# Output projections by seven products: the weights' sums on VectorE and stored in two parts, sums of y partly by accumulating DMAs, y loaded by the GpSimd queue

## The chip, the cores and the metric

One core of a Trainium2 chip runs the whole program. It has five engines, each with its own queue of instructions that it works through in order: TensorE (PE, with PEld for its weight loads), VectorE (DVE), ScalarE (ACT), GpSimd (POOL) and SyncE (SP). The metric is the time of one execution in microseconds; the median of three runs is quoted.

## The reference, cut to what matters

Two pre-norm residual layers on x of 1024 tokens by 1024 channels, and a final norm. Each ends in one projection of 2048 channels to 1024:

```
# layer 0: two branches, concatenated, one output projection
y_a = u * sg * silu(za)                            # gMLP, channels 0..1023
y_b = (layernorm(ht * sigmoid(og)) + skip * xc) * silu(zb)   # mLSTM, 1024..2047
x = x + concatenate([y_a, y_b], axis=-1) @ w_out
# layer 1: differential attention with 16 heads of 128 channels
o = rmsnorm(o, subln_g) * (1 - lam_init)
x = x + (o.reshape(seq, 2048) * silu(z)) @ w_out
return rmsnorm(x, final_g)
```

## The kernel before, in words

Every fp32 product is made of three passes on TensorE: an operand is split into a high part (a cast on ScalarE, L94) and a low part (a subtraction on VectorE, L95), and high by high, low by high and high by low are added. A tile of weights is loaded raw from memory (`wr`, L72) by SP's queue, 512 KB at a time into two buffers, and split into `wh` and `wl`. A matmul of 128x512 follows the one before it after about 0.23 us at the full clock, and after 0.43 us at half of it.

Both output projections are done by seven products of half size instead of eight (Winograd's form of Strassen's scheme). The activations are held as tiles `a[half, k, i]`, each 128x1024: half is the token half, k the channel half, i one of four pairs of 128 channels. Written for short, a11 is half 0, k 0; a21 is half 1, k 0; a12 is half 0, k 1; a22 is half 1, k 1. The products run in the order 1, 7, 2, 6, 5, 3, 4, and each takes 96 matmuls of 128x512. Product 1 needs a11; 7 needs s3 = a11 − a21 (L338); 2 needs a12; 6 needs a21 + a22 − a11 (L341, L342), 5 a21 + a22, 3 a12 less that (L344), 4 a22. These sums run on GpSimd. The weights' sums (products 7, 6, 5, 4) depend on the weights alone: `wout_sums` makes them on GpSimd during layer 0's gMLP stage (L292 to L295) from `wb` tiles that SP's queue loads (L290), and GpSimd's queue stores them to memory (`td`, L297). The output projections load them back through L72 like other weights, and split them there.

In layer 0 the activations lie in memory (`yd`): channels 0 to 1023 are stored by the gMLP stage, channels 1024 to 2047 by the tail of the mLSTM (L1118). In layer 1 they are the heads' outputs (`wd`), and each is multiplied on VectorE (L330) by a row of scales that is loaded into 128 partitions (`yr`, L329, two buffers). Part of product 1 runs, in each layer, as a filler in gaps of the stage before. Product 1's result p (`p`, evacuated at L372) is added to the accumulator tiles `xa` on GpSimd (L398, L400), as soon as those are loaded with the residual (L389).

The gMLP stage goes by eight groups of 128 channels, twice: u (L1187, and the spatial matmul sp, L1190, which needs the normalised va of L1174; the result `yu` at L1192 and L1195), and za (L1207, L1208). Its matmuls stand at L133. A call of `wout_sums` stands behind every second group in the code.

A scheduler reorders all instructions, so the order on an engine is not that of the code; what stands in an engine's queue, and what it waits for, is fixed when the kernel is built. Each DMA that GpSimd issues waits for one of eight slots, that is for the DMA eight places ahead of it in that queue. `SLOTS` says at which of an attention head's steps the last two heads run fillers; once these are done, the fillers of the output projection come.

Of the kernel before, what the change touches and what calls it, by code (L numbers as in the profile page):

```python
# [9 lines left out]
F32 = mybir.dt.float32  # L10
F32R = mybir.dt.float32r
# [3 lines left out]
ALU = mybir.AluOpType  # L15
# [3 lines left out]
P = 128  # L19
# [6 lines left out]
AH, BH, CH = 8, 4, 16  # L26
# [8 lines left out]
SLOTS = {14: (0, 5, 6, 7), 15: (1, 3, 4, 6)}  # L35
# [9 lines left out]
class Trunk:  # L45
# [106 lines left out]
    def run(self):  # L152
        tc, nc, io = self.tc, self.nc, self.io
        with tc.tile_pool(name="const", bufs=1) as cp, \
# [41 lines left out]
            w = self.load_w(io["wO"][1], w0, 1)  # L196
# [18 lines left out]
            w = [self.next_w(), None]  # L215
# [35 lines left out]
            odd.release()  # L251
            self.xp = pool("x3acc", side="right")
            p = pool("wout1b")
            self.wout_rest(p)
            self.wout_p1()
            self.wout_evac(7)
            for i in range(4):
                for k in range(2):
                    self.wout_load(p, k, 1, (i,))
# [24 lines left out]
    def wout_sums(self, pool, layer, i):  # L284

        nc, sub = self.nc, ALU.subtract
        b11, b12, b21, b22 = (pool.tile([P, 1024], F32, name=f"wb{j}", tag=f"wb{j}") for j in range(4))
        t2 = pool.tile([P, 1024], F32, name="wt2", tag="wt2")
        for j, b in enumerate((b11, b12, b22, b21)):
# [27 lines left out]
    def wout_load(self, pool, half, k, pairs):  # L317

        nc = self.nc
        hs = slice(half * 512, (half + 1) * 512)  # L320
        for i in pairs:
            x = self.a[half, k, i] = pool.tile([P, 2, 512], F32, name=f"a{half}{k}{i}")
            for n in range(2):
                nc.sync.dma_start(out=x[:, n], in_=(self.y if self.layer == 0 else self.w)[8 * k + 2 * i + n][:, hs])
            if self.layer == 1:
                r = self.ytmp.tile([P, 2, 512], F32, name="yr", tag="t3", bufs=2)
                for n in range(2):
                    kb = 8 * k + 2 * i + n
                    nc.sync.dma_start(out=r[:, n], in_=self.rr[kb:kb + 1, hs].broadcast_to([P, 512]))  # L329
                nc.vector.tensor_tensor(out=x, in0=x, in1=r, op=ALU.mult)  # L330

    def wout_lhs(self, n, i):

        g, sub = self.nc.gpsimd.tensor_tensor, ALU.subtract
# [10 lines left out]
        return {1: a11, 2: a12, 3: a12, 4: a22, 5: a21, 6: a11}[n]  # L345

# [7 lines left out]
    def wout_prod(self, n, tiles=range(4), groups=((0,), (1,), (2,), (3,))):  # L354

        x = "A" if n in (1, 2, 5, 3) else "B"
        for grp in groups:
            parts = []
            for i in grp:
                w = self.load_w(self.wsrc[n][i])  # L360
                parts.append((i, self.split_y(self.wout_lhs(n, i)), [a.rearrange("p (k c) -> p k c", k=2) for a in w]))
# [758 lines left out]
    def gmlp(self, new_pool):  # L1120
# [56 lines left out]
        wsp = new_pool("w_sums", side="right")  # L1177
        yu = []
        for g in range(AH):
# [16 lines left out]
            if g % 2:  # L1196
                self.wout_sums(wsp, 0, g // 2)
        ap.release()
        mixa = new_pool("mixa")
        for g in range(AH):  # L1200
# [9 lines left out]
            if g % 2:  # L1210
                self.wout_sums(wsp, 1, g // 2)
# [88 lines left out]
```

## Time and profile before

| | |
|---|---|
| median of 3 runs | 2244.39 us (2243.82 to 2246.65) |
| profiled execution | 2249.3 us, of which span 2247.5 us |
| TensorE busy | 2103.8 us, 94% |
| VectorE busy | 1537.3 us, 68% |
| ScalarE busy | 998.0 us, 44% |
| GpSimd busy | 415.6 us, 18% |
| granted TensorE clock, mean | 0.964 |

The profile is of one execution. The span is what the trace covers; 1.8 us of the time lie outside it. The page cuts the span into 40 slices of 56.2 us and gives a tenth per slice: slices 3 to 6 hold the gMLP stage (129 to 355 us), slices 14 to 16 layer 0's output projection (from about 760 us), slices 36 to 40 that of layer 1. "Busy" of the TensorE counts a matmul's whole passage, which overlaps with the next one's.

### The profile page before, as it was taken

What the parts mean: (1) busy time and instruction counts of PE and PEld (TensorE: products, weight loads), DVE (VectorE), ACT (ScalarE), POOL (GpSimd) and SP (SyncE); (2) the same over time, 40 slices, a digit from 0 to 9 for tenths busy, and PEclk for the clock granted to TensorE, in tenths of its full rate; (3) what the DMA queues carried; (4) which work ended last, traced back from release to release, by engine and by line L of the source; (5) the groups of instructions that cost most, each with busy time, mean ns of one, the idle gap of its engine ahead of it and who ended that gap; (6) DMA issues with size and microseconds to landing.
All of it is one profiled execution on the core that took longest, in us unless ns stands there. A gap on an engine that the chain in (4) does not pass through costs nothing. (4 is left out here: it accounts for less than half of the span.)

```text
span 2247.5 us, 32307 instructions
## 1 busy us (share of the span) xinstructions
PE 2103.8 (94%) x11594; PEld 1803.5 (80%) x11594; DVE 1537.3 (68%) x3113; ACT 998.0 (44%) x1943; POOL 415.6 (18%) x427
## 2 busy tenths in 40 slices
PE   8889799999999859999999999999999999997398
PEld 7878688988989737878888888888888888876286
DVE  6363324577777777657777777777777777888665
ACT  5411113343434423544555555555555555663143
POOL 0065600000000273101111111111111111114810
PEclk9989899999999969999999999999999999998699
DMA  4456632121123443445443444454444444347523
GB/s 165 144 208 230 212 117 97 39 71 48 62 66 99 159 168 112 139 132 143 120 119 100 116 115 120 112 130 105 114 115 111 113 124 114 90 146 242 183 95 122
DMA packets 109749, 281.81 MB, mean 125 GB/s; under 512 B 21348, under 2 KB 22276, under 8 KB 109588
## 3 DMA queue, kind: packets, MB, share of 16 engines
q1 hardware_dynamic: 89972, 225.07, 33.4%
q0 software_dynamic: 19616, 54.68, 7.6%
q8 instruction: 91, 1.49, 0.3%
q14 instruction: 70, 0.57, 0.1%
HBM read 168.32 MB, written 44.20 MB: 95 GB/s over the span
## 5 line engine op out<-in xcount | busy, mean ns | idle before, releaser
L133 PE MATMUL un<-hh,wh 128*128 128x512 f32 x1240 | 493.8, 398 | 15.7 <-ACT u L1187 14.5
L133 PE MATMUL un<-hh,wl 128*128 128x512 f32 x1240 | 493.5, 398 | 1.6 <-DVE wl L95 1.6
L133 PE MATMUL un<-hl,wh 128*128 128x512 f32 x1240 | 490.6, 396 | 0.0
L95 DVE TENSOR_TENSOR wl<-wr,wh 128x1024 fp32r<-128x1024 f32 (+1 forms) x191 | 262.1, 1374 | 207.3 <-ACT wh L94 197.8
L94 ACT CAST wh<-wr 128x1024 fp32r<-128x1024 f32 (+1 forms) x191 | 199.8, 1048 | 283.2 <-PE un L133 174.7
L133 PEld LDWEIGHTS un<-hh,wh 128*128 128x128 f32 x1240 | 235.7, 190 | 63.0 <-ACT u L1187 15.3
L133 PEld LDWEIGHTS un<-hh,wl 128*128 128x128 f32 x1240 | 235.1, 190 | 52.4 <-DVE wl L95 2.8
L133 PEld LDWEIGHTS un<-hl,wh 128*128 128x128 f32 x1240 | 235.1, 190 | 48.2
L643 ACT ACTIVATE p<-p,mn 128x128 f32<-128x128 f32 (+7 forms) x256 | 197.7, 774 | 121.1 <-DVE mn L640 120.8
L640 DVE CUSTOM_DVE_ANT_0 p<-S,mask 128x128 f32<-128x128 f32 (+7 forms) x256 | 184.8, 750 | 3.4 <-PE tp L667 1.9
L148 PE MATMUL un<-wh,hh 128*128 128x256 f32 (+1 forms) x560 | 161.4, 289 | 5.0 <-ACT wh L94 3.0
L148 PE MATMUL un<-wl,hh 128*128 128x256 f32 (+1 forms) x560 | 160.2, 286 | 0.9 <-DVE wl L95 0.8
L148 PE MATMUL un<-wh,hl 128*128 128x256 f32 (+1 forms) x560 | 160.2, 286 | 0.4 <-DVE hl L95 0.4
L366 PE MATMUL wps<-wh,yh 128*128 128x512 f32 x320 | 128.3, 406 | 18.2 <-ACT yh L94 15.1
L366 PE MATMUL wps<-wl,yh 128*128 128x512 f32 x320 | 129.8, 406 | 9.2 <-DVE wl L95 9.0
L95 DVE TENSOR_TENSOR yl<-a,yh 128x1024 fp32r<-128x1024 f32 x56 | 85.1, 1521 | 70.3 <-ACT yh L94 70.1
L94 ACT CAST yh<-a 128x1024 fp32r<-128x1024 f32 x56 | 58.6, 1047 | 165.6 <-PE wps L366 130.7
L694 POOL DMA_DIRECT2D wd<-wt x64 | 36.7, 574 | 510.2 <-DVE wt L692 485.6
L366 PE MATMUL wps<-wh,yl 128*128 128x512 f32 x320 | 128.7, 403 | 1.1 <-DVE yl L95 1.1
L95 DVE TENSOR_TENSOR PT<-tp,PT 128x512 fp32r<-128x512 f32 (+1 forms) x192 | 106.0, 552 | 33.0 <-ACT PT L94 32.9
L681 PE MATMUL O<-PT,Vh 128*128 128x512 f32 x320 | 113.7, 388 | 0.5 <-ACT mr L707 0.5
L148 PEld LDWEIGHTS un<-wh,hh 128*128 128x128 f32 x560 | 108.4, 194 | 6.5 <-ACT wh L94 3.2
(339 smaller groups left out, 4698.4 us busy)
## 6 DMA issues: line engine op xcount, KB each, us to landing
wr<-wO SPq DMA_DIRECT2D x79, 512.0 KB
wr<-wE SPq DMA_DIRECT2D x46, 512.0 KB
wr<-td SPq DMA_DIRECT2D x32, 512.0 KB
sw<-xs SPq DMA_DIRECT2D x256, 64.0 KB
Qh<-xh SPq DMA_DIRECT2D x128, 128.0 KB
Ql<-xl POOLq DMA_DIRECT2D x128, 128.0 KB, 4.0
td<-wb POOLq DMA_DIRECT2D x24, 512.0 KB, 5.9
wb<-wF SPq DMA_DIRECT2D x16, 512.0 KB
```

The lines of the kernel that those rows point to most:

```text
L94: return (self.nc.scalar.copy(out=out_h, in_=src).ins, self.nc.vector.tensor_tensor(out=out_l, in0=src, in1=out_h.bitcast(F32), op=ALU.sub ...
L95: self.nc.vector.tensor_tensor(out=out_l, in0=src, in1=out_h.bitcast(F32), op=ALU.subtract).ins)
L133: nc.tensor.matmul(out=ps, lhsT=a[:, kb, :], rhs=b[:, kb, :], start=(kb == 0 and i == 0), stop=(kb == KB - 1 and i == 2))
L148: nc.tensor.matmul(out=ps, lhsT=a[:, k0 + k, sl], rhs=b, start=start and k == i == 0, stop=stop and k == n - 1 and i == 2)
L366: self.nc.tensor.matmul(out=self.wps[x, t], lhsT=y[a][:, k, t * P:(t + 1) * P], rhs=w[b][:, k, :], start=n in (1, 7, 5) and i == k == j == ...
L640: nc.vector.tensor_tensor_reduce(out=p[:, :W], in0=S[:, :W], in1=self.mask[:, T - W:], scale=-0.125, scalar=1e30, op0=ALU.add, op1=ALU.min ...
L643: nc.scalar.activation(out=p[:, :W], in_=p[:, :W], func=AF.Exp, scale=-1.0, bias=mn, accum_out=s)
L681: mm(out=O.rearrange("p (a t) -> p a t", a=2)[:, :, a0:], lhsT=Vh, rhs=pt, start=s == 0, stop=False)
L694: nc.gpsimd.dma_start(out=self.w[h][:, js], in_=wt)
```

## The change

- `wout_sums`: 16 calls with half tiles (128x512) instead of 8 with whole ones, one behind every group; the four sums run on VectorE (L300 after) instead of GpSimd, and each sum is split at once into its high and low part (ScalarE and VectorE, L94 and L95), which are stored as two tiles of 256 KB each (L304). What is stored doubles, from 16.8 to 33.5 MB. The weights' loads go to GpSimd's queue (L289, 256 KB each, two buffers).
- `wout_rhs`: products 7, 6, 5 and 4 load the two parts (L363, 512 KB each) straight into the buffers of `wh` and `wl`, or into a pair of raw ones, and split nothing.
- the sums of y: s3 on VectorE; a21 + a22 and a12 + a11 by DMAs that add to their destination (`accum_op`, L349, L351; 512 KB each, four of each in a layer); a11 − (a21 + a22) on VectorE, with the sign turned so that the next is a sum.
- product 1's p is added to `xa` by twelve accumulating DMAs of 256 KB in each layer (L415) instead of eight GpSimd instructions.
- y's loads (L333) go by GpSimd's queue, but for layer 1's a11 and a21, which stay on SP's; the scales `yr` (L337) go by GpSimd's.
- the order of these steps in the code, and `SLOTS`.

```diff
-SLOTS = {14: (0, 5, 6, 7), 15: (1, 3, 4, 6)}
+SLOTS = {14: (0, 3, 5, 6, 7), 15: (1, 3, 4)}
...
-            self.td = [[dp.tile([4, P, 1024], F32, name=f"td{l}{j}") for j in range(4)] for l in range(2)]
+            self.td = [[dp.tile([4, 2, P, 1024], F32, name=f"td{l}{j}") for j in range(4)] for l in range(2)]
...
             self.wout_load(p, 1, 0, range(4))
+            self.wout_load(p, 0, 1, range(3))
             self.wout_rest(p)
+            self.wout_ps(range(4), "B")
             self.wout_p1()
-            for k in (1, 0):
-                self.wout_load(p, k, 1, range(3))
-            self.wout_ps(range(4), "B")
             run(self.wout_prod(7))
-            for k in (0, 1):
-                self.wout_load(p, k, 1, (3,))
+            self.wout_load(p, 0, 1, (3,))
+            self.wout_load(p, 1, 1, range(4))
...
+    def wout_fetch(self, pool, n):
...
+            for j in (0, 1, 3, 2):
+                self.nc.gpsimd.dma_start(out=self.wb[j], in_=src[4 * j + n % 8 // 2][:, cs])
+
+    def wout_sums(self, pool, n):
...
-            nc.sync.dma_start(out=b, in_=self.io["wF" if layer == 0 else "wG"][4 * (0, 1, 3, 2)[j] + i])
-        g = nc.gpsimd.tensor_tensor
-        g(out=b11, in0=b12, in1=b11, op=sub)
-        g(out=t2, in0=b22, in1=b11, op=sub)
-        g(out=b12, in0=b22, in1=b12, op=sub)
-        g(out=b21, in0=b21, in1=t2, op=sub)
-        for j, b in enumerate((b11, t2, b12, b21)):
-            nc.gpsimd.dma_start(out=self.td[layer][j][i], in_=b)
+        b11, b12, b21, b22 = self.wb
+        self.wout_fetch(pool, n + 1)
...
+        v = nc.vector.tensor_tensor
+        for j, (out, x, y, op) in enumerate(((b11, b12, b11, sub), (t2, b11, b22, sub), (b12, b22, b12, sub), (b21, b21, t2, ALU.add))):
+            v(out=out, in0=x, in1=y, op=op)
+            parts = [pool.tile([P, 512], F32R, name=f"wt{x}", tag=f"wt{x}", bufs=3) for x in "hl"]
+            self.split2(*parts, out)
+            for x, part in enumerate(parts):
+                nc.gpsimd.dma_start(out=self.td[n // 8][j][n % 8 // 2, x][:, cs], in_=part.bitcast(F32))
...
+        q = nc.sync if k == 0 and self.layer == 1 else nc.gpsimd
...
-                nc.sync.dma_start(out=x[:, n], in_=(self.y if self.layer == 0 else self.w)[8 * k + 2 * i + n][:, hs])
+                q.dma_start(out=x[:, n], in_=(self.y if self.layer == 0 else self.w)[kb + n][:, hs])
...
-                    nc.sync.dma_start(out=r[:, n], in_=self.rr[kb:kb + 1, hs].broadcast_to([P, 512]))
+                    nc.gpsimd.dma_start(out=r[:, n], in_=self.rr[kb + n:kb + n + 1, hs].broadcast_to([P, 512]))
...
-            g(out=s3, in0=a11, in1=a21, op=sub)
+            v(out=s3, in0=a11, in1=a21, op=sub)
             return s3
         if n == 6:
-            g(out=a21, in0=a21, in1=a22, op=ALU.add)
-            g(out=a11, in0=a21, in1=a11, op=sub)
-        if n == 3:
-            g(out=a12, in0=a12, in1=a11, op=sub)
+            g(out=a21, in_=a22, accum_op=ALU.add)
+            v(out=a11, in0=a11, in1=a21, op=sub)
+            g(out=a12, in_=a11, accum_op=ALU.add)
...
+    def wout_rhs(self, n, i):
+
+        src = self.wsrc[n][i]
+        if n in (1, 2, 3):
+            w = self.load_w(src)
+        else:
+            w = [self.wp.tile([P, 1056], F32R, name="wr", tag="r4", bufs=2)[:, :1024] if i == 1 else
+                 self.wp.tile([P, 1024], F32R, name=x, tag=x, bufs=2) for x in ("wh", "wl")]
+            for x, part in zip(w, (src[0], src[1])):
+                self.nc.sync.dma_start(out=x.bitcast(F32), in_=part)
...
-        g, add = self.nc.gpsimd.tensor_tensor, ALU.add
         for t in range(4):
-            x = self.xa[t + 4].rearrange("p (a c) -> p a c", a=2)
-            g(out=x, in0=x, in1=self.p1[t].unsqueeze(1).broadcast_to([P, 2, 512]), op=add)
-            x = self.xa[t][:, 512:]
-            g(out=x, in0=x, in1=self.p1[t], op=add)
+            for x in (self.xa[t][:, 512:], self.xa[t + 4][:, 512:], self.xa[t + 4][:, :512]):
+                self.nc.gpsimd.dma_start(out=x, in_=self.p1[t], accum_op=ALU.add)
...
-            if g % 2:
-                self.wout_sums(wsp, 0, g // 2)
+            self.wout_sums(wsp, g)
```

On SP's queue in the gMLP stage of layer 0, before; `wb` are the raw tiles for the weights' sums, `wr` the weights of the stage's own groups:

```order
L290 DMA wb_1841<-wF 128x1024
L290 DMA wb_2009<-wF 128x1024
L72 DMA wr<-wE 128x1024
L290 DMA wb_2006<-wF 128x1024
L290 DMA wb_2007<-wF 128x1024
L290 DMA wb_2008<-wF 128x1024
L72 DMA wr<-wE 128x1024
L290 DMA wb_2176<-wF 128x1024
```

And the same stretch of SP's queue after:

```order
L856 DMA dw<-gw 32x128
L866 DMA eb<-dnM 128x1024
L853 DMA decB<-ddec 128x32
L866 DMA eb<-dnM 128x1024 x3
L72 DMA wr<-wE 128x1024 x20
```

Before, three or four `wb` loads stand ahead of each weight load of a group; after, the weight loads stand alone, and the `wb` loads are on GpSimd's queue, among the stores of the sums. On VectorE's queue of the changed kernel the first four calls' sums stand ahead of the last of the normalisations that make va (here `av`; `wt`, `wtl` are a sum and its low part):

```order
L300 TENSOR_TENSOR wb_1829<-wb_1830,wb_1829 128x512
L65 TENSOR_TENSOR ar_t<-ar_t,ar_h 128x8
L95 TENSOR_TENSOR wtl<-wb_1719,wth 128x512
L66 SCALAR_TENSOR_TENSOR ar_y<-ar_t,ar_y 128x8
L300 TENSOR_TENSOR wt_1949<-wb_1829,wb_1832 128x512
L64 TENSOR_TENSOR ar_t<-ar_y 128x8
L300 TENSOR_TENSOR wb_1830<-wb_1832,wb_1830 128x512
L65 TENSOR_TENSOR ar_t<-ar_t,ar_h 128x8
L95 TENSOR_TENSOR wtl<-wb_1829,wth 128x512
L66 SCALAR_TENSOR_TENSOR ar_y<-ar_t,ar_y 128x8
L300 TENSOR_TENSOR wb_1831<-wb_1831,wt_1949 128x512
L1189 TENSOR_SCALAR av_255<-av_255,amv,ar_y 128x1024
```

Before, nothing of `wout_sums` is on VectorE; from the first piece of the third call to the first `av` now stand thirteen pieces of 128x512 that were not there. On GpSimd's queue at layer 0's output projection, before (`p` is product 1's result, `yd_79` and `yd_80` are the last channels of the mLSTM, `s` is s3):

```order
L400 TENSOR_TENSOR xa_7375<-xa_7375,p_7104 128x512
L398 TENSOR_TENSOR xa_7380<-xa_7380,p_7344 128x1024
L400 TENSOR_TENSOR xa_7376<-xa_7376,p_7344 128x512
L398 TENSOR_TENSOR xa_7381<-xa_7381,p_7352 128x1024
L400 TENSOR_TENSOR xa_7377<-xa_7377,p_7352 128x512
L1118 DMA yd_79<-xc 128x512
L1118 DMA yd_80<-xc 128x512
L338 TENSOR_TENSOR s_7429<-a_6499,a_7362 128x1024
```

After, at the same place (`a_7818` to `a_7827` are a21):

```order
L415 DMA xa_7841<-p_7800 128x512
L415 DMA xa_7845<-p_7800 128x512 x2
L415 DMA xa_7842<-p_7808 128x512
L415 DMA xa_7846<-p_7808 128x512
L1133 DMA yd_79<-xc 128x512
L415 DMA xa_7846<-p_7808 128x512
L1133 DMA yd_80<-xc 128x512
L333 DMA a_7818<-yd_65 128x512
L333 DMA a_7818<-yd_66 128x512
L333 DMA a_7821<-yd_67 128x512
```

The twelve additions are DMAs now, and a21's loads, which stood on SP's queue behind four loads of `td`, stand behind them and behind the last two stores of `yd`. On SP's queue in layer 1's output projection, before, the last five of the 25 rows from product 1's last weights to those of product 2:

```order
L329 DMA yr<-rrd 128x512 x2
L324 DMA a_20856<-wd_8642 128x512
L324 DMA a_20856<-wd_8643 128x512
L329 DMA yr<-rrd 128x512 x2
L72 DMA wr<-wG 128x1024 x4
```

After:

```order
L407 DMA xa_21231<-x2d 128x1024
L407 DMA xa_21227<-x2d 128x1024
L409 DMA gB<-fg 128x1024
L72 DMA wr<-wG 128x1024 x4
L363 DMA wr<-td_87 128x1024 x2
```

The weights of product 2 now stand right behind the residual's loads; a12, a22 and their `yr` are on GpSimd's queue.

## Rows read from the trace of the kernel before

**Rows 1.** The page's slices: PE's busy tenths.

```profile
PE   8889799999999859999999999999999999997398
```

**Rows 2.** Windows of the gMLP stage: length; each engine's busy us (instructions); clock; DMA.

```profile
129.00:151.00 22.00, 15.01 (x50) 11.08 (x49) 19.39 (x26) 0.98 (x2) 12.62 (x8) 0.69 0.64 232
151.00:211.00 60.00, 60.00 (x301) 49.99 (x300) 26.63 (x23) 10.71 (x15) 37.03 (x23) 1.00 0.57 198
211.00:272.00 61.00, 46.50 (x194) 37.35 (x194) 19.39 (x16) 7.49 (x10) 32.47 (x21) 0.86 0.69 239
...
190.00:200.00 10.00, 10.00 (x53) 8.40 (x52) 4.32 (x5) 2.14 (x3) 1.20 (x1) 1.00 1.01 357
```

**Rows 3.** Waits of 129 to 355 us: us in total, times, longest.

```profile
ACT wh L94 <- DMA wr<-wE: 51.9, 3, 20.3
```

**Rows 4.** Timeline of SP's queue there: start, duration, instruction.

```profile
240.09 20.23 SPq L290 DMA_DIRECT2D wb<-wG  x4
```

**Rows 5.** Timeline of VectorE there.

```profile
135.09 12.36 DVE L1174 TENSOR_SCALAR av<-av,amv,ar_y 128x1024 f32<-128x1024 f32 x8
```

**Rows 6.** Groups by line, 129 to 355 us: count, busy us, mean ns, idle.

```profile
L1195 DVE TENSOR_TENSOR yu<-yu,u 128x512 f32<-128x512 f32 x16 | 22.5, 1407 | 1.7
...
L292 POOL TENSOR_TENSOR wb<-wb,wb 128x1024 f32<-128x1024 f32 x7 | 16.6, 2368 | 65.2 <-DMA wb<-wG 37.5 <-DMA wb<-wF 27.7
```

**Rows 7.** Timeline of PE in layer 0's projection, with the idle time before.

```profile
773.00 0.50 PE L366 MATMUL wps<-wl,yh 128*128 128x512 f32 x1 [4.25 <-DVE wl L95]
...
810.28 0.80 PE L366 MATMUL wps<-wh,yh 128*128 128x512 f32 x1 [15.10 <-ACT yh L94]
```

**Rows 8.** Windows there, of L366's matmuls alone: PE, PEld, clock, DMA.

```profile
800.00:844.50 44.50, 28.86 (x97) 22.17 (x98) 0.72 0.55 196
...
820.00:830.00 10.00, 10.00 (x44) 7.98 (x43) 1.00 0.28 95
```

**Rows 9.** Timeline there: VectorE, GpSimd, SP's queue.

```profile
785.46 7.24 DVE L1106 TENSOR_SCALAR og<-og,mv,lr_y 128x256 f32<-128x256 f32 x4
...
794.05 0.69 DVE L1117 TENSOR_TENSOR xc<-xc,zb 128x512 f32<-128x512 f32 x1
...
785.29 2.36 POOL L398 TENSOR_TENSOR xa<-xa,p 128x1024 f32<-128x1024 f32 x1 [11.21 <-ACT p L372]
...
798.01 0.54 POOL L1118 DMA_DIRECT2D yd<-xc  x1 [2.41 <-DVE xc L1117]
...
777.66 21.53 SPq L72 DMA_DIRECT2D wr<-td  x4
799.29 5.60 SPq L324 DMA_DIRECT2D a<-yd  x8
```

**Rows 10.** Timeline of PE in layer 1's projection, with the idle time before.

```profile
2116.86 1.22 PE L366 MATMUL un<-wh,yh 128*128 128x512 f32 x2 [34.32 <-ACT wh L94]
2122.33 0.80 PE L366 MATMUL un<-wl,yh 128*128 128x512 f32 x1 [4.24 <-DVE wl L95]
```

**Rows 11.** Windows there, of L366 alone.

```profile
2033.00:2082.00 49.00, 39.05 (x155) 30.61 (x156) 0.86 0.68 236
...
2116.50:2146.90 30.40, 25.79 (x102) 20.45 (x103) 0.85 0.26 86
2146.90:2247.00 100.10, 89.76 (x380) 71.68 (x378) 0.96 0.31 111
```

**Rows 12.** Timeline of SP's queue there.

```profile
2072.66 0.91 SPq L324 DMA_DIRECT2D a<-wd  x2
...
2110.04 15.91 SPq L72 DMA_DIRECT2D wr<-wG  x4
```

**Rows 13.** DMA issues: KB each, median us from issue to landing.

```profile
Ql<-xl POOLq DMA_DIRECT2D x128, 128.0 KB, 4.0
td<-wb POOLq DMA_DIRECT2D x24, 512.0 KB, 5.9
```

**Rows 14.** Windows of layer 1's first loads, all engines as in Rows 2.

```profile
2010.00:2020.00 10.00, 6.81 (x22) 5.36 (x23) 8.99 (x22) 5.09 (x14) 1.08 (x2) 0.66 0.99 326
```

More of the change, by code (lines that the diff above doesn't have):

```diff
@@ L251, in run @@
             odd.release()
+            p = pool("wout1b")
             self.xp = pool("x3acc", side="right")
-            p = pool("wout1b")
+            self.wout_load(p, 0, 1, range(4))
             self.wout_rest(p)
             self.wout_p1()
+            self.wout_load(p, 1, 1, range(4))
             self.wout_evac(7)
-            for i in range(4):
-                for k in range(2):
-                    self.wout_load(p, k, 1, (i,))
             for n in (2, 6, 5, 3):
@@ L276, in run @@
             self.wp.release()
-    def wout_sums(self, pool, layer, i):
-        nc, sub = self.nc, ALU.subtract
-        b11, b12, b21, b22 = (pool.tile([P, 1024], F32, name=f"wb{j}", tag=f"wb{j}") for j in range(4))
-        t2 = pool.tile([P, 1024], F32, name="wt2", tag="wt2")
-        for j, b in enumerate((b11, b12, b22, b21)):
-            nc.sync.dma_start(out=b, in_=self.io["wF" if layer == 0 else "wG"][4 * (0, 1, 3, 2)[j] + i])
-        g = nc.gpsimd.tensor_tensor
-        g(out=b11, in0=b12, in1=b11, op=sub)
-        g(out=t2, in0=b22, in1=b11, op=sub)
-        g(out=b12, in0=b22, in1=b12, op=sub)
-        g(out=b21, in0=b21, in1=t2, op=sub)
-        for j, b in enumerate((b11, t2, b12, b21)):
-            nc.gpsimd.dma_start(out=self.td[layer][j][i], in_=b)
+    def wout_fetch(self, pool, n):
+        if n < 16:
+            src = self.io["wF" if n < 8 else "wG"]
+            cs = slice(n % 2 * 512, (n % 2 + 1) * 512)
+            self.wb = [pool.tile([P, 512], F32, name=f"wb{j}", tag=f"wb{j}", bufs=2) for j in range(4)]
+            for j in (0, 1, 3, 2):
+                self.nc.gpsimd.dma_start(out=self.wb[j], in_=src[4 * j + n % 8 // 2][:, cs])
+    def wout_sums(self, pool, n):
+        nc, sub = self.nc, ALU.subtract
+        b11, b12, b21, b22 = self.wb
+        self.wout_fetch(pool, n + 1)
+        cs = slice(n % 2 * 512, (n % 2 + 1) * 512)
+        t2 = pool.tile([P, 512], F32, name="wt2", tag="wt2")
+        v = nc.vector.tensor_tensor
[5 more added lines that the diff above has]
+                nc.gpsimd.dma_start(out=self.td[n // 8][j][n % 8 // 2, x][:, cs], in_=part.bitcast(F32))
     def wout_start(self, layer, pool):
@@ L320, in wout_load @@
         hs = slice(half * 512, (half + 1) * 512)
+        q = nc.sync if k == 0 and self.layer == 1 else nc.gpsimd
         for i in pairs:
             x = self.a[half, k, i] = pool.tile([P, 2, 512], F32, name=f"a{half}{k}{i}")
+            kb = 8 * k + 2 * i
             for n in range(2):
-                nc.sync.dma_start(out=x[:, n], in_=(self.y if self.layer == 0 else self.w)[8 * k + 2 * i + n][:, hs])
+                q.dma_start(out=x[:, n], in_=(self.y if self.layer == 0 else self.w)[kb + n][:, hs])
             if self.layer == 1:
@@ L327, in wout_load @@
                 for n in range(2):
-                    kb = 8 * k + 2 * i + n
-                    nc.sync.dma_start(out=r[:, n], in_=self.rr[kb:kb + 1, hs].broadcast_to([P, 512]))
+                    nc.gpsimd.dma_start(out=r[:, n], in_=self.rr[kb + n:kb + n + 1, hs].broadcast_to([P, 512]))
                 nc.vector.tensor_tensor(out=x, in0=x, in1=r, op=ALU.mult)
     def wout_lhs(self, n, i):
-        g, sub = self.nc.gpsimd.tensor_tensor, ALU.subtract
+        g, v, sub = self.nc.gpsimd.dma_start, self.nc.vector.tensor_tensor, ALU.subtract
         a11, a21, a12, a22 = (self.a.get((h, k, i)) for k in range(2) for h in range(2))
@@ L337, in wout_lhs @@
             s3 = self.ytmp.tile([P, 2, 512], F32, name="s3", tag="t3", bufs=2)
-            g(out=s3, in0=a11, in1=a21, op=sub)
+            v(out=s3, in0=a11, in1=a21, op=sub)
             return s3
         if n == 6:
-            g(out=a21, in0=a21, in1=a22, op=ALU.add)
-            g(out=a11, in0=a21, in1=a11, op=sub)
-        if n == 3:
-            g(out=a12, in0=a12, in1=a11, op=sub)
+            g(out=a21, in_=a22, accum_op=ALU.add)
+            v(out=a11, in0=a11, in1=a21, op=sub)
+            g(out=a12, in_=a11, accum_op=ALU.add)
         return {1: a11, 2: a12, 3: a12, 4: a22, 5: a21, 6: a11}[n]
+    def wout_rhs(self, n, i):
[7 more added lines that the diff above has]
+                self.nc.sync.dma_start(out=x.bitcast(F32), in_=part)
+        return [x.rearrange("p (k c) -> p k c", k=2) for x in w]
     def split_y(self, raw):
@@ L359, in wout_prod @@
             for i in grp:
-                w = self.load_w(self.wsrc[n][i])
-                parts.append((i, self.split_y(self.wout_lhs(n, i)), [a.rearrange("p (k c) -> p k c", k=2) for a in w]))
+                parts.append((i, self.split_y(self.wout_lhs(n, i)), self.wout_rhs(n, i)))
             for t in tiles:
@@ L1177, in gmlp @@
         wsp = new_pool("w_sums", side="right")
+        self.wout_fetch(wsp, 0)
         yu = []
@@ L1209, in gmlp @@
             nc.gpsimd.dma_start(out=self.y[g], in_=yu[g])
-            if g % 2:
-                self.wout_sums(wsp, 1, g // 2)
+            self.wout_sums(wsp, AH + g)
         wsp.release()
```

## Prediction

> **What bounds the kernel now.** I read the page's slices first, to see where TensorE pauses, and then for each such stretch the windows, the waits and the timelines of the queues. TensorE is busy nine tenths or more nearly everywhere, and three of its dips lie where the change works [rows 1]. So the question is how much time TensorE loses in three places, and how much of that goes.
>
> *The gMLP stage.* From 151 to 211 us TensorE is full: 301 matmuls in 60.0 us, 5.0 per us. At that pace the 50 matmuls of 129 to 151 us are 10 us of work, and the 194 of 211 to 272 us are 39 us [rows 2]: 12 and 22 us are lost. The 22: ScalarE waits three times, 51.9 us in all, for a group's own weights [rows 3]. They are late because SP's queue stood for 20.23 us at four loads of `wb` [rows 4], whose buffers GpSimd's sums still held, and the next weight load stands behind those. The 12: eight normalisations of va take 12.36 us on VectorE, and the spatial matmul needs them all [rows 5]. GpSimd takes 2.37 us per sum, and VectorE's products of 128x512 take 1.41 us in the mean of this stage [rows 6]; with GpSimd idle one takes 0.69 [rows 9].
>
> *Layer 0's projection.* TensorE stalls 4.25 us at 773 us for a low part, and 15.10 us before product 7 starts at 810.28 [rows 7]. At full clock 44 matmuls pass in 10 us, 0.227 us each; so the 97 of 800 to 844.5 us are 22.0 us of work, and 22.5 us are lost, at a mean clock of 0.72 [rows 8]. On the queues one sees why: four normalisations on VectorE take 7.24 us beside GpSimd's additions of product 1; the last mLSTM store is issued only at 798.01; and SP issues a21's loads at 799.29, behind four weight loads that stood 21.53 us [rows 9].
>
> *Layer 1's projection.* Between product 1 and product 2 TensorE is idle for 34.32 us and, after two matmuls, for 4.24 more [rows 10]. From 2033 to 2082 us are 155 matmuls, 35.2 us of work: 13.8 lost. From 2116.5 to 2146.9 are 102, 23.2 us: 7.2 lost, at a mean clock of 0.85. What follows product 2 takes 100.1 us and is close to full [rows 11]. In the idle stretch SP issues the loads of a12, a22 and their scales, from 2072.66 on, each pair of scales waiting for a buffer that VectorE frees; product 2's weights are issued after them all, at 2110.04 [rows 12]. In sum 13.8 + 34.3 + 7.2 = 55 us are lost there.
>
> **The change, part by part.**
>
> *gMLP.* SP's queue holds the groups' weights alone, so the 22 us lose their cause. In its place stands the load on the DMA engines: 16 calls of 1 MB read and 2 MB stored are 50 MB, and VectorE's order spreads them from the end of va to za's third group, by the windows some 170 us. With 6 MB of weights that is 330 GB/s; the best window of this stage moved 357 [rows 2]. I take 7 us of waiting for that and a gain of 15; the bounds are 22 (none shows) and 5. VectorE's own share: eight pieces a call at 0.69 us, 5.5 us, so 88 us in all; in 151 to 211 us it is busy 26.6 of 60 today [rows 2], with about half of that owed to GpSimd. ScalarE adds 64 casts of 128x512; even at the mean 0.71 us of its fifteen instructions in that window they are 46 us, and it is busy 10.7 of 60. Both fit, if stores don't hold them up. Against it stands va: thirteen pieces, 9 us, come ahead of the eight normalisations; GpSimd's sums leave, which by the 1.55 us of each normalisation against 1.38, twice the 0.69 of half the size [rows 9], and by steps before them that stand beside GpSimd as well, I take to give back 5. So 4 us lost there (bounds 0, and 14 if their loads are late as well). Net 11 gained, between 22 and −9.
>
> *Layer 0.* GpSimd computes nothing there any more. The four normalisations at a quarter to a half of 7.24, the stall of 4.25 and the other stretched steps bring the tail forward by about 10 us. From the last store to product 7's first matmul it takes 12.3 us now (798.01 to 810.28); after, the store, one pair's loads (256 KB landed in about 2 to 4 us for others), s3 and a cast, about 8: 4 gained. In product 7 itself 12 us are lost now (34.2 us from 810.28 to 844.5 for 22.0 of work); I leave 3 for the low clock after the pause: 9 gained. Product 2's small stalls beside GpSimd give 2. Together 25. This isn't the reordering that the code suggests: on GpSimd's queue a21's loads stand behind the additions of p and the last two stores, so they can't go before the mLSTM ends. The last six of these additions wait for product 1's evacuation (GpSimd's third now starts at 785.29 after a wait for it [rows 9]); if 1.5 MB of them take more than some 10 us, a21 is late by the excess. Bounds 10 and 35 (all of 22.5, 10 and 2).
>
> *Accumulating DMAs.* No row shows one. Both nearest rows are of GpSimd's queue: 128 KB from on-chip to on-chip memory in 4.0 us, 512 KB to main memory in 5.9 [rows 13]. With 8 at once on their way I take what the stage can move, and as the lower bound one after another at the second row's rate, 89 GB/s; a21 + a22, 2.1 MB, takes 7 to 24 us then. In layer 0 product 6 begins two products of 22 us after a21's loads, so both fit; in layer 1 they stand in the sum below.
>
> *Weights in two parts.* 32 splits on ScalarE and VectorE leave, and 1 MB instead of 512 KB is loaded for each group of 24 matmuls, 5.5 us: 190 GB/s, under what other stretches move. Off the path; nothing gained or lost, unless the loads behind the change's other transfers are late.
>
> *Layer 1.* Product 2's weights now stand right behind the residual's loads, y's second half goes by the other queue, VectorE runs without GpSimd beside it, the additions of a's leave GpSimd. So none of the 55 us keeps its cause, and product 6 could start at 2147 − 55 = 2092. But the transfers stay: from 2034 us to there a12, a22, their scales, product 7's and 2's weights, half of 1's, two groups of 6's, the residual, 3.1 MB of p and 2.1 of a22 to add, 27 MB. At the 326 GB/s of the layer's first loads [rows 14] that is 83 us, to 2117. Some of product 7's weights come earlier, so I take 2110: 37 gained, between 20 (326 GB/s, and each accumulation counted double, for what it reads of its destination) and 55. The last head's shift in `SLOTS` I cost at nothing within these bounds: the same matmuls, in other gaps.
>
> The rule of the Trainium skill that speaks against this part is in "DMA: Bandwidth & Descriptors", section "Issuing engines are not separate DMA queues": transfers run on the same 16 DMA engines whichever engine starts them, so a second queue saves only the time of issuing. By it alone layer 1's sixteen moved loads of y, at 0.45 us each, would be worth 7 us instead of 37. The trace shows more than issuing at stake: SP stood 21.53 us at four loads [rows 9], a wait of the queue and not of the DMA engines.
>
> *Sum.* −11 − 25 − 37 = −73 us. Against the profiled execution's own 2249.3 us that is 2176; this execution is 4.9 us above the median of the runs, so I forecast 2171.
>
> **The rivals.**
>
> *The DMA engines bind.* The stored sums double, GpSimd's additions become transfers, and nothing is read less. Then the gMLP stage gains nothing (330 GB/s asked at 2 KB rows, which moved 326 in layer 1), layer 0 gains 20 and layer 1 only 25: −45, 2199. For it: both stretches at 0.9 to 1.0 of the DMA engines' time [rows 2, 14]. Against it: in the idle 34 us of layer 1 the queue waited, not the DMA engines. By the Trainium skill's rule above, this is how it goes too.
>
> *All causes go, no new ones come.* 20, 33 and 55: −108, 2136. For it: TensorE has no other work to wait for. Against it: 27 MB in 58 us is 465 GB/s, which no window shows.
>
> *Layer 0 stays held.* The head of GpSimd's queue waits for product 1's evacuation and the mLSTM's last store; if VectorE's tail doesn't shorten, because it was the sequence of small steps and not GpSimd that set it, a21 comes as late as now and the change doesn't do there what it says: layer 0 gives 8, in all −56, 2188.
>
> *Slower: accumulating DMAs.* If they run one after another at the rate of the 128 KB row, 33 GB/s, the last 1.5 MB of p take 47 us from about 783, and a21's loads are issued at 830 us instead of 799: 31 lost, less 15 of product 7 and 2. In layer 1 3.1 MB of p and 2.1 of a22 take 160 us from about 2050, and the 2.1 MB of a12's sum another 64: product 3 starts at 2274 instead of 2147 + 44 = 2191, 83 late. 11 − 16 − 83 = −88 gained, 2332. It decides from about 48 GB/s down: there layer 0 gains nothing, and product 3 starts at 2202.
>
> **How the numbers follow.** Chances: the forecast 0.47, with its own range of 2155 to 2190; the DMA engines bind 0.21; nothing new comes 0.12; layer 0 stays held 0.12; accumulating DMAs slow 0.08. The range has to hold eight in ten: from 2132, which takes in most of the third case, up to 2212, the upper side of the second; only the last case and parts of the others lie outside. A change within 0.2%, 4.5 us and about what a measurement here can tell, needs the DMA case and slow additions together: 0.03. Slower 0.07, what is left of the last case; faster 0.90.
>
> **What would show it.** Right: in the gMLP stage no ScalarE wait for `wr<-wE`, at most some 20 us of pauses; product 7 of layer 0 starting at 790 to 800 us on this trace's scale less the first gain, with no TensorE wait for a low part in it; in layer 1 the pause before product 2 under 8 us, and whatever is left before product 6, ended by L349. Wrong: waits of VectorE for `td` stores ahead of `yu` or `av` (the first term); twelve L415 transfers that take over 10 us each, with a21's loads behind them (the second); windows of layer 1 at a DMA share near 1.0 while TensorE waits (the third). The forecast fails by most if the accumulations are slow, since both projections wait for them.

## The result

| | before | after |
|---|---|---|
| median | 2244.27 us (2243.82 to 2246.65, 4 runs) | 2229.49 us (2228.83 to 2231.76, 4 runs) |
| span of the profiled execution | 2247.5 us | 2227.4 us |

The ratio of after to before is 0.9934 (95% interval 0.9917 to 0.9951): 15 us faster, where 73 were forecast and the range began at 32. The changed kernel's page, slices of TensorE, of its granted clock and of the DMA engines, each in tenths of 55.7 us:

```profile
PE   8899899999999859999999999999999999987687
...
PEclk9999999999999979999999999999999999988799
DMA  4488952111123696545444344444434444366964
```

The dip in the gMLP stage (slices 3 to 6) is shallower than in [rows 1], that of layer 0's projection (14, 15) is still there, with the DMA engines at 9 tenths in slice 15. In slices 37 to 40 TensorE still pauses, with the DMA engines at 6, 9, 6 and 4.

To see where the time came from I took six places in each trace. Microseconds from the start of the span:

| place | before | after | lead |
|---|---|---|---|
| last activation of za (end of gMLP) | 355.2 | 346.9 | 8.3 |
| last transposition of the mLSTM's tail | 794.1 | 774.9 | 19.2 |
| layer 0, product 7's first matmul | 810.3 | 799.4 | 10.9 |
| first rotary copy `xs` of layer 1 | 980.2 | 959.5 | 20.7 |
| last head's last store of `wd` | 2035.8 | 2027.3 | 8.5 |
| end of the span | 2247.5 | 2227.4 | 20.1 |

So the gMLP stage gave 8, the mLSTM's tail 11, layer 0's products 10. The pause before product 7 took 8 back, and layer 1 gave nothing: its attention's tail lost 12, and what follows won 12.

The pause in layer 0, timelines of the changed kernel for TensorE, VectorE and GpSimd:

```profile
799.41 0.80 PE L384 MATMUL wps<-wh,yh 128*128 128x512 f32 x1 [23.84 <-ACT yh L94]
...
797.00 2.50 DVE L346 TENSOR_TENSOR s<-a,a 128x1024 f32<-128x1024 f32 x2 [19.91 <-DMA a<-yd]
...
783.11 0.55 POOL L333 DMA_DIRECT2D a<-yd  x1 [0.88 <-DMA xa<-p]
785.71 0.55 POOL L333 DMA_DIRECT2D a<-yd  x1 [2.05 <-DMA xa<-p]
788.31 0.55 POOL L333 DMA_DIRECT2D a<-yd  x1 [2.05 <-DMA xa<-p]
790.92 0.55 POOL L333 DMA_DIRECT2D a<-yd  x1 [2.06 <-DMA xa<-p]
792.27 0.55 POOL L333 DMA_DIRECT2D a<-yd  x1 [0.81 <-DMA yd<-xc]
796.08 4.30 POOL L333 DMA_DIRECT2D a<-yd  x8 [3.26 <-DMA yd<-xc]
```

TensorE waits 23.84 us where it waited 15.10 [rows 7]. VectorE waits 19.91 for a21. And a21's loads are at first issued one every 2.6 us, because each has to wait until one more of p's accumulating DMAs has landed and freed its slot. That is 256 KB per 2.6 us, 101 GB/s. The last loads of a21 wait for the slots of the two mLSTM stores (`yd<-xc`), plain transfers that stand among the additions: they land after 13.0 and 15.5 us here, after 2.3 and 4.7 before. The DMA issues of the changed kernel (KB each, median us to landing):

```profile
a<-a POOLq DMA_DIRECT2D x16, 512.0 KB, 9.9
...
xa<-p POOLq DMA_DIRECT2D x24, 256.0 KB, 10.1
```

In layer 1 the windows are these (TensorE, its weight loads, VectorE, ScalarE, GpSimd, clock, DMA share, GB/s):

```profile
2030.00:2050.00 20.00, 20.00 (x89) 16.44 (x88) 12.48 (x24) 5.30 (x6) 7.03 (x13) 1.00 0.76 278
2050.00:2070.00 20.00, 11.45 (x37) 8.60 (x36) 11.61 (x11) 7.03 (x7) 9.83 (x15) 0.73 1.04 369
2070.00:2090.00 20.00, 8.03 (x25) 5.75 (x24) 7.72 (x10) 6.20 (x7) 9.78 (x14) 0.67 1.09 279
2090.00:2120.00 30.00, 22.23 (x89) 17.26 (x87) 18.83 (x19) 7.61 (x12) 11.42 (x14) 0.90 1.02 283
```

From 2050 us on the DMA engines are full, and at the same share they move 369 GB/s in one window and 279 in the next. VectorE's timeline shows whom it hits, TensorE's what follows:

```profile
2077.12 0.69 DVE L424 TENSOR_TENSOR xa<-xa,wps 128x512 f32<-128x512 f32 x1 [6.51 <-DMA xa<-p]
...
2083.78 1.23 DVE L338 TENSOR_TENSOR a<-a,yr 128x1024 f32<-128x1024 f32 x1 [4.83 <-DMA yr<-rrd]
...
2086.70 2.35 DVE L95 TENSOR_TENSOR wl<-wr,wh 128x1024 fp32r<-128x1024 f32 x2
...
2087.98 0.80 PE L384 MATMUL un<-wl,yh 128*128 128x512 f32 x1 [8.40 <-DVE wl L95]
...
2122.98 0.77 PE L384 MATMUL wps<-wh,yh 128*128 128x512 f32 x1 [10.09 <-DMA wh<-td]
```

VectorE works in order: it waits for an accumulation and for a row of scales, and the split of product 2's weights, ready behind them, is late. Product 6 then waits 10.09 us for weights in two parts, and not for the sum of L349 that the prediction named.

### The profile page after: what moved, and what is told of

Same layout as the page of the kernel before. It is cut to its first block, busy times and chain, and to the rows that moved or that the text cites. A ratio compares the mean times of both kernels' runs of the same rounds, so it can differ in the third digit from the quotient of the medians.

```text
span 2227.4 us, 32820 instructions
## 1 busy us (share of the span) xinstructions
PE 2100.5 (94%) x11594; PEld 1802.0 (81%) x11594; DVE 1504.0 (68%) x3225; ACT 1004.3 (45%) x1975; POOL 366.2 (16%) x627
## 5 line engine op out<-in xcount | busy, mean ns | idle before, releaser
L95 DVE TENSOR_TENSOR wl<-wr,wh 128x1024 fp32r<-128x1024 f32 (+1 forms) x159 | 196.0, 1234 | 130.3 <-ACT wh L94 129.3
L94 ACT CAST wh<-wr 128x1024 fp32r<-128x1024 f32 (+1 forms) x159 | 166.3, 1047 | 191.1 <-PE un L133 125.6
L384 PE MATMUL wps<-wh,yh 128*128 128x512 f32 x264 | 106.4, 408 | 38.0 <-ACT yh L94 23.8
L95 DVE TENSOR_TENSOR PT<-tp,PT 128x512 fp32r<-128x512 f32 (+1 forms) x192 | 106.2, 553 | 34.6 <-ACT PT L94 34.3
L94 ACT CAST yh<-a 128x1024 fp32r<-128x1024 f32 x56 | 58.4, 1047 | 157.0 <-PE wps L384 124.3
L95 DVE TENSOR_TENSOR yl<-a,yh 128x1024 fp32r<-128x1024 f32 x56 | 70.7, 1263 | 85.4 <-ACT yh L94 85.3
L384 PE MATMUL wps<-wl,yh 128*128 128x512 f32 x264 | 108.5, 411 | 10.7 <-DVE wl L95 9.1
L94 ACT CAST PT<-tp 128x512 fp32r<-128x512 f32 (+1 forms) x192 | 91.7, 477 | 49.7 <-PE tp L682 47.2
```

The costliest lines, as they stand in the source:

```text
L94: return (self.nc.scalar.copy(out=out_h, in_=src).ins, self.nc.vector.tensor_tensor(out=out_l, in0=src, in1=out_h.bitcast(F32), op=ALU.sub ...
L95: self.nc.vector.tensor_tensor(out=out_l, in0=src, in1=out_h.bitcast(F32), op=ALU.subtract).ins)
L384: self.nc.tensor.matmul(out=self.wps[x, t], lhsT=y[a][:, k, t * P:(t + 1) * P], rhs=w[b][:, k, :], start=n in (1, 7, 5) and i == k == j == ...
```

## The experiments

Two theories were put against each other. One: adding during a transfer is dear in itself, and so the accumulating DMAs cost what the forecast lost. Two: the DMA engines are full of ordinary bytes, and it doesn't matter who adds. Beside them stood the places where `yr`, the last projection and the raw weights are issued. Ends of spans and medians can differ by some us from run to run. The gMLP stage alone, whose code is the same in nine of these kernels, ended between 340.2 and 346.9 us, on average at 343.7: a stage's time in a single profile is no surer than that.

**p added on VectorE.**

```diff
-                self.nc.gpsimd.dma_start(out=x, in_=self.p1[t], accum_op=ALU.add)
+                self.nc.vector.tensor_tensor(out=x, in0=x, in1=self.p1[t], op=ALU.add)
```

> Product 1's p is added to the accumulator tiles by twelve VectorE instructions of 128x512 per layer instead of twelve accumulating DMAs; all else as changed. If the accumulating DMAs hold a21 (their slots free one after another, 2.6 us each, ahead of a21's loads), layer 0's pause before product 7 falls from 23.8 us to about 10, and layer 1's pauses of 8.4 and 10.1 us shrink as well: 2229 becomes 2208 to 2218. If the DMA engines are simply full with loads, only 3.1 MB of moved bytes go, and the pause falls by less than 5 us: 2222 to 2230.

Measured: 2209.89 us, ratio to before 0.986 (95% interval 0.9838 to 0.9882). The pause before product 7:

```profile
785.73 0.80 PE L384 MATMUL wps<-wh,yh 128*128 128x512 f32 x1 [10.80 <-ACT yh L94]
```

23.84 became 10.80, and the span from layer 1's first `xs` to the end 1259.3 instead of 1267.9 us. That is the first theory's number, and 20 us in all (17 by the ratios) for twelve transfers of 256 KB per layer. In layer 1 only one of the two pauses shrank as expected: the 10.1 us before product 6 became 1.3, but the 8.4 before product 2 became 12.1, and VectorE, which now adds p too, ends it.

**p copied instead of added**, to part the adding from the bytes.

```diff
-                self.nc.gpsimd.dma_start(out=x, in_=self.p1[t], accum_op=ALU.add)
+                self.nc.gpsimd.dma_start(out=x, in_=self.p1[t])
```

> The twelve transfers of p per layer copy onto the accumulator tile instead of adding to it (the residual is lost there, so the sum is left out); same bytes from p, same queue, same order. If the adding is what makes them slow (10.1 us from issue to landing for 256 KB, where a plain 256 KB store lands in 2.3 to 3.6), they land in under 5 us and layer 0's pause before product 7 falls to 12 to 17 us. If it is the crowd on the DMA engines, they land in 8 to 10 us and the pause stays above 20.

Measured, in a single run: 2211.16 us, a pause of 16.69 us, and landings (median) of

```profile
xa<-p POOLq DMA_DIRECT2D x24, 256.0 KB, 7.4
```

The landing is at neither theory's number: 7.4 us, so most of the 10.1 isn't the adding. But with the same transfers in the same places the time is 18 us less, and the pause is within the first theory's range. The window from 760 to 800 us shows it too; first the changed kernel, then this one:

```profile
760.00:800.00 40.00, 12.83 (x53) 9.49 (x53) 16.68 (x42) 6.33 (x8) 16.28 (x25) 0.70 1.05 316
```

```profile
760.00:800.00 40.00, 19.97 (x76) 14.51 (x75) 20.75 (x42) 8.44 (x9) 19.97 (x35) 0.74 1.02 393
```

At full DMA engines 316 GB/s move with the additions and 393 without. An added byte takes more of the engines' time than a copied one. An estimate of how much: 12.6 MB moved in these 40 us with the additions, 3.1 of them added, and 15.7 MB without; if the whole difference is theirs, an added byte took about as long as two copied ones.

**No accumulating DMA at all**: the sums of y on VectorE too.

```diff
-            g(out=a21, in_=a22, accum_op=ALU.add)
+            v(out=a21, in0=a21, in1=a22, op=ALU.add)
             v(out=a11, in0=a11, in1=a21, op=sub)
-            g(out=a12, in_=a11, accum_op=ALU.add)
+            v(out=a12, in0=a12, in1=a11, op=ALU.add)
```

> No accumulating DMA is left: p's additions and the three sums of y (a21 + a22, its difference, a12 + a11) are all on VectorE; all else as changed. With p alone there it was 2210. If adding during a transfer is dear in itself, product 6 of layer 1 starts earlier (its a21 + a22 took 7.6 us for each 512 KB), and the time is 2198 to 2207. If layer 1 waits for y's loads and scales and not for sums, it stays at 2208 to 2214.

Measured: 2199.30 us, ratio 0.9805 (0.9784 to 0.9827), 10.6 less than with p alone. Together the accumulating DMAs cost 30 us of the changed kernel's time. For the sums of y, adding and bytes went together; only for p does a run part them.

**The scales of layer 1's a11 and a21 on SP's queue**, on the changed kernel and on the version without accumulating DMAs:

```diff
-                    nc.gpsimd.dma_start(out=r[:, n], in_=self.rr[kb + n:kb + n + 1, hs].broadcast_to([P, 512]))
+                    (nc.sync if k == 0 else nc.gpsimd).dma_start(out=r[:, n], in_=self.rr[kb + n:kb + n + 1, hs].broadcast_to([P, 512]))
```

> The scales yr of a11 and a21 in layer 1 are loaded by SP's queue again, each pair behind its a tile, all else as changed. If yr comes late because sixteen loads of a stand ahead of it on the DMA engines (first yr 8.5 us, VectorE's multiplications hold the attention's work behind them), the attention's tail shortens by 5 to 10 us: 2219 to 2224. If the 8.4 MB take their time in any order, nothing moves by more than 3 us.

> As the version without accumulating DMAs, and the scales of a11 and a21 in layer 1 on SP's queue. If yr's place behind the attention's stores and its pairing with a matter by themselves, 4 to 6 us less than that version, as in the run on the changed kernel (2223 against 2229). If all of it was transfers that wait for each other, within 2 us of it.

Measured: 2223.12 us (ratio 0.9913, 0.9898 to 0.9928), and 2197.38 us (0.9795, 0.9773 to 0.9817). In the profiles the attention ends 8.5 and 6.3 us earlier, at 2018.8 and 2005.7. On the changed kernel 5 to 6 us of it arrive (by the ratios and by the medians), as the first expectation says; without accumulations only 2, less than the intervals can tell.

**SLOTS as before**, on the changed kernel and on the last version:

```diff
-SLOTS = {14: (0, 3, 5, 6, 7), 15: (1, 3, 4)}
+SLOTS = {14: (0, 5, 6, 7), 15: (1, 3, 4, 6)}
```

> SLOTS as before the change, all else as changed. If the last projection's place, two attention steps earlier, starves TensorE in the attention's tail (51 us from the last projection matmul to the last head's store, against 34 before), that stretch falls to about 38 us and the time by 5 to 10 us: 2219 to 2224. If the projection behind it is bound by its transfers, y's loads start 5 us later and the gain is taken back: 2227 to 2235.

> SLOTS as before the change on the version without accumulating DMAs and with a's scales on SP's queue (2197). On the changed kernel SLOTS as before shortened the attention's tail by 7 us and lost 12 behind it. If it lost them to transfers that accumulations made longer, now 2190 to 2196; if to the later start of y's loads as such, 2198 to 2204.

Measured: 2232.16 us (0.9950, 0.9933 to 0.9966), as the first text's second case says, and 2194.85 us (0.9777, 0.9762 to 0.9791), as the second text's first case says. On the changed kernel the attention's tail ended 6.9 us earlier, and all of it was lost again behind it (product 6 at 2127.41 instead of 2122.98). Without accumulations 2.5 us are left, within the two intervals. The step that the forecast costed at nothing was worth some 7 us in its place. That the transfers behind it decide whether this arrives fits the two traces, but neither difference in the time is clear of noise.

**Fewer bytes in layer 1**: no scales for a12 and a22, on the version without accumulating DMAs.

```diff
-            if self.layer == 1:
+            if self.layer == 1 and k == 0:
                 r = self.ytmp.tile([P, 2, 512], F32, name="yr", tag="t3", bufs=2)
```

> As the version without accumulating DMAs; the scales of a12 and a22 in layer 1 are neither loaded nor multiplied (that part of the computation is left out): 4.2 MB of transfers and eight VectorE instructions less. If the transfers bind layer 1's projection, product 2 starts 8 to 12 us earlier and the time falls by as much, to about 2195; if VectorE's own work or TensorE bound it, by less than 4 us.

Measured, in a single run: 2183.50 us, 16 less. The windows of the two versions, first with the scales:

```profile
2030.00:2050.00 20.00, 10.06 (x39) 7.97 (x38) 8.22 (x9) 5.55 (x6) 7.43 (x14) 0.75 1.03 400
2050.00:2070.00 20.00, 9.74 (x33) 6.40 (x31) 18.02 (x22) 8.21 (x9) 7.05 (x13) 0.76 0.87 328
```

```profile
2030.00:2050.00 20.00, 14.99 (x50) 10.40 (x49) 13.52 (x15) 9.18 (x10) 5.08 (x10) 0.83 1.03 402
2050.00:2070.00 20.00, 16.11 (x59) 12.15 (x58) 18.27 (x21) 7.29 (x9) 0.00 (x0) 0.83 0.34 114
```

About 400 GB/s is what the stage moves when it is full; with fewer bytes the full stretch ends some 10 us earlier and TensorE has its work: 59 matmuls instead of 33 in the second window. The eight multiplications that also went are about 10 us of VectorE, so this run doesn't part the bytes from VectorE's work.

**The raw weights on SP's queue**, all else as changed.

```diff
-                self.nc.gpsimd.dma_start(out=self.wb[j], in_=src[4 * j + n % 8 // 2][:, cs])
+                self.nc.sync.dma_start(out=self.wb[j], in_=src[4 * j + n % 8 // 2][:, cs])
```

> The raw weights of the sums are loaded by SP's queue as before the change, all else as changed. If SP's queue, where the groups' weights stand behind them, was what cost 22 us in the gMLP stage before, most of the stage's gain of 8.3 us goes: 2235 to 2240. If the gain came from VectorE without GpSimd beside it, it stays: 2228 to 2232.

Measured: 2233.95 us (0.9967, 0.9952 to 0.9982), a little below the first expectation. The gMLP stage ends at 356.2 us instead of 346.9: all that it had gained goes. Some of these 9 us are made up in layer 1. SP's queue waits in the gMLP stage (us in all, times, longest):

```profile
SPq L289 <- DVE wtl L95: 73.5, 35, 4.5
SPq L72 <- DVE wl L95: 63.2, 11, 17.9
```

L289 are the raw weights, and they wait for buffers that VectorE's splits free; the groups' own weights, L72, stand behind them. Yet these aren't what is missing here: as in the changed kernel, the trace has no ScalarE wait for `wr<-wE`. TensorE waits for ScalarE's `u`, 18.0 us against 6.6 in the changed kernel, and ScalarE's queue is held ahead of it by the casts of the sums (from 129 to 272 us):

```profile
PE un L133 <- ACT u L1203: 18.0, 8, 4.0
...
ACT wth L94 <- DVE wb L300: 38.8, 11, 5.0
```

So the run shows that the gain hangs on the queue of the raw weights. It doesn't show that it does so through late weights of the groups.

**Sums stored whole**, on the changed kernel and on the version without accumulating DMAs:

```diff
-            parts = [pool.tile([P, 512], F32R, name=f"wt{x}", tag=f"wt{x}", bufs=3) for x in "hl"]
-            self.split2(*parts, out)
-            for x, part in enumerate(parts):
-                nc.gpsimd.dma_start(out=self.td[n // 8][j][n % 8 // 2, x][:, cs], in_=part.bitcast(F32))
+            nc.gpsimd.dma_start(out=self.td[n // 8][j][n % 8 // 2][:, cs], in_=out)
```

> The sums of weights are stored whole (256 KB per sum and call) and split after they are loaded again, as before the change; all else as changed. 16.8 MB of stores, 16.8 MB of loads, 64 casts and 64 subtractions in the gMLP stage less, and 32 splits of 128x1024 in the projections more. If the doubled stores are what kept the gMLP stage at a gain of 8 us instead of 11 to 20, it gains 6 to 10 more, and layer 1, bound by transfers, a few: 2212 to 2222. If the splits in the projections come on the path, or VectorE's order with av sets the stage, 2226 to 2235.

> The same on the version without accumulating DMAs and with a's scales on SP's queue (2197). If transfers bind both stages, 2180 to 2190; if VectorE, which does all sums there, becomes the bound with the splits, 2195 to 2205.

Measured: 2212.21 us (0.9851, 0.9835 to 0.9868), and 2198.14 us (0.9791, 0.9777 to 0.9806). The first is 17 us less than the changed kernel, though not for the expected reason: the gMLP stage ends at 346.4, no earlier than with two parts. From the start of product 7 in layer 0 to layer 1's `xs` it takes 158.1 instead of 160.1 us, in layer 1 11 us less (1256.8 from `xs` to the end). That fits a second part whose bytes cost only where the accumulations had filled the DMA engines: without these, whole sums and sums in two parts (2197.38) come out the same. It also means that the 30 us of the accumulations aren't theirs alone: with whole sums, taking them away and moving `yr` gives 14 us (2212.21 to 2198.14).

**What is left of the change when all this is taken out**: whole sums and SLOTS as before, no accumulating DMA, a's scales on SP's queue.

> No accumulating DMA, a's scales on SP's queue, SLOTS as before the change, and the weights' sums stored whole and split again: what is left of the change is the sums on VectorE, the queues, and the order of the steps. The version with two parts and SLOTS as before was 2195, the one with whole sums and SLOTS as changed 2198. If whole sums cost nothing once no DMA adds, and SLOTS is worth 2 to 3 us, 2193 to 2198; if the splits on VectorE come on the path of the shorter attention tail, 2199 to 2206.

Measured: 2201.67 us (0.9823, 0.9809 to 0.9836), as the second expectation says, and slower than the same with two parts (2194.85, 0.9777): 7 us by the medians, 10 by the ratios. With SLOTS as changed the two were equal. Why isn't settled: I ran no version that parts the splits' place from their number.

## Why the prediction was wrong

*gMLP, 11 forecast, 8.3 measured: near in size, its cause shown only in part.* No ScalarE wait for `wr<-wE` is left, against 51.9 us [rows 3], and with the raw weights back on SP's queue the gain is gone; so it didn't come from VectorE without GpSimd beside it alone. That late weights had cost the 22 us isn't shown: in that run they aren't waited for either. And the `wb` buffers behind which the weights stood were held by GpSimd's sums only in part: in the profile of before SP's queue waited 60.0 us for these and 65.4 for the stores of their results. By the nine profiles of this stage the gain is 8 to 15 us, on average 11.5, against one profile of before; that it meets the forecast is in part luck, since the two halves went otherwise than I split them. Windows after:

```profile
129.00:151.00 22.00, 18.28 (x80) 14.80 (x79) 18.10 (x41) 6.79 (x11) 11.74 (x20) 0.92 0.92 320
151.00:211.00 60.00, 58.07 (x286) 48.02 (x285) 44.97 (x67) 19.01 (x31) 32.05 (x60) 1.00 0.83 275
211.00:272.00 61.00, 51.33 (x219) 41.05 (x218) 40.43 (x60) 21.63 (x34) 32.80 (x62) 0.92 0.90 311
```

Against [rows 2] the first window holds 80 matmuls instead of 50, 6 us more work at 5 per us, where I had forecast 4 us lost; the third 219 instead of 194, only 5 us of the 15 forecast; the second loses 3. The doubled stores, for which I took 7 us, do hold the stage: ScalarE's casts of the sums wait for them, and `u` and `z`, for which TensorE waits 13.3 us, stand behind these casts:

```profile
ACT wth L94 <- DMA td<-wth: 57.2, 24, 7.7
...
PE un L133 <- ACT z L1222: 6.7, 2, 4.9
PE un L133 <- ACT u L1203: 6.6, 4, 2.6
```

With whole sums these waits of TensorE are gone, but others take their place, for va and for `yu` on VectorE (11.4 and 10.7 us on the changed kernel; shown is the version without accumulations), and the stage ends no earlier:

```profile
PE sp L1203 <- DVE av L1186: 10.3, 1, 10.3
PE sp L1203 <- DVE yu L1205: 8.5, 3, 3.8
```

*Layer 0, 25 forecast, 12.4 measured.* The tail came forward by 10.9 us beyond the stage before it, as the forecast's 10; the products lost 10 us less, against 9 + 2. The step that failed is the one on accumulating DMAs: "With 8 at once on their way I take what the stage can move". They freed their slots every 2.6 us, near the lower bound of 89 GB/s that I had named and not taken. a21's loads stood behind them, as the text said they would; the last 1.5 MB of additions, six times 2.6 us, needed 16 us and not some 10, and with the two stores among them took the pause from 15.1 to 23.8 us instead of shortening it by 4. Done on VectorE the pause is 10.80. Without any accumulating DMA, layer 1's first `xs` comes 34.6 us earlier than before (945.6 us), where the forecast for both stages was 36: apart from that step the first two terms hold.

*Layer 1, 37 forecast, −0.6 measured.* Four steps failed. The first is the same: the sum of 27 MB at 326 GB/s counted an added byte as a copied one, though full windows after moved 279 to 369 GB/s where full windows without additions moved 393 to 402. Taking the additions away gave layer 1 14.7 us (1253.2 from `xs` to the end). The second is `yr` of a11 and a21 on another queue than its a, not costed at all, and SLOTS, costed "at nothing within these bounds". The attention's tail from layer 1's `xs` to the last store is 12 us longer than before; `yr` back on SP's queue takes 7.6 of that away, and SLOTS as before 6.7. Of what `yr` costs there, 5 to 6 us reach the end of the changed kernel; of what SLOTS costs, none. The third is the weights in two parts, put "Off the path" unless other transfers make them late. Just this came true: product 6 waits 10.09 us for them, and stored whole the changed kernel is 17 us faster.

The fourth is "none of the 55 us keeps its cause". Without accumulating DMAs layer 1 gains 14.1 us of the 37, and 18.1 in the fastest version. The pause before product 2, which was to be under 8 us, is 8.40 in the changed kernel and still 8.74 without accumulations and with a's scales on SP's queue. There VectorE ends it: multiplications by scales, `xa` sums and the additions of p, which this version has put there, stand ahead of the split of product 2's weights:

```profile
2060.41 1.90 DVE L415 TENSOR_TENSOR xa<-xa,p 128x512 f32<-128x512 f32 x3 [0.28 <-ACT p L390]
2063.57 2.48 DVE L338 TENSOR_TENSOR a<-a,yr 128x1024 f32<-128x1024 f32 x2 [1.27 <-DMA yr<-rrd]
2065.96 2.47 DVE L424 TENSOR_TENSOR xa<-xa,wps 128x512 f32<-128x512 f32 x4
...
2069.49 1.22 DVE L95 TENSOR_TENSOR wl<-wr,wh 128x1024 fp32r<-128x1024 f32 x1
```

Of the rivals, "the DMA engines bind" describes layer 1 best, where the engines are full from 2050 us on. Its figure, 2199, is 30 us off: it too priced an addition as a copy, and it gave the gMLP stage no gain. For that stage it also claimed a DMA share of 0.9 to 1.0, which in [rows 2] only the window of 10 us has; the longer ones stand at 0.57 to 0.69. "Accumulating DMAs slow" was right on the cause, and its sign, twelve transfers of over 10 us with a21's loads behind them, came true in the median (10.1); it was wrong on the rate, 33 GB/s, where about 100 was measured, and on the 48 from which it was to decide.

The Trainium skill's "DMA: Bandwidth & Descriptors" says in "Issuing engines are not separate DMA queues" that transfers run on the same 16 DMA engines whichever engine starts them, and that a second queue saves only the time of issuing. The trace agrees with the first: from 2050 to 2070 us loads of SP's queue and of GpSimd's are on their way together, at a DMA share of 1.04. With the second the measurement differs: the same raw weights on SP's queue instead of GpSimd's end the gMLP stage 9.3 us later, more than the 6.7 us by which its nine profiles with unchanged code differ.

The sum of what the runs took away: 30 us of accumulations, 2 of `yr`, 2.5 of SLOTS. The version without accumulating DMAs, a's scales on SP's queue and SLOTS as before is the fastest of those that compute everything: 2194.85 us, 0.9777 of before, 35 us below the changed kernel. From there to the forecast of 2171 some 24 us stay open; by the profiles it is layer 1 that falls short. The run without a12's and a22's scales shows that these transfers and their multiplications are worth about 16 there; but the forecast had counted them among its 27 MB, so what the open part is isn't shown.

## What to carry to other kernels

Before work is moved from an engine to transfers, add up the bytes of the stretch in which they will run, and price an addition during a transfer well above a copy: here the same sums on VectorE were 30 us faster. A load that starts a product must not stand behind slow transfers in a queue with few slots. When one stage is full, a change ahead of it can show in its start and not in the end: read each place in the trace by itself. And when a cost is taken away, look at what is waited for next: whole sums freed ScalarE in the gMLP stage, and VectorE became the wait.

## What I had not expected of the hardware

Beside full DMA engines, an accumulating DMA of 256 KB between on-chip tiles landed after 10.1 us (median of 24), and one freed its slot every 2.6 us; the same transfer as a copy landed after 7.4. One of 512 KB took 9.9. Plain stores of 256 KB behind the additions landed after 13.0 and 15.5 us, behind copies in their place after 9.1 and 10.3. GpSimd's instruction that issues an accumulating DMA took 0.86 us or more, where a plain one takes 0.55:

```profile
809.42 0.89 POOL L349 DMA_DIRECT2D a<-a  x1 [1.95 <-DVE yl L95]
```
